# Sliding windows on one Trainium2 core: a second batch half stored four elements further on, and tiles that leave by two queues

## The chip, the cores and the metric

The kernel runs on one core of a Trainium2 chip. The metric is the device time of one launch in microseconds (us), median of the runs. Before the change it was 185.79 us over three runs (185.7 to 185.88). The profile is of one execution that took 186.0 us, of which the instruction span is 184.2 us.

The engines that matter here are VectorE (DVE in the profile), ScalarE (ACT), GpSimd (POOL) and SyncE (SP). POOL and SP issue the transfers; POOL writes the descriptors of its own in software (queue q0 in the profile), SP and ACT have theirs generated by hardware (q1 and q10). All transfers run on the same sixteen DMA engines of the core.

## The reference

```python
n_h = (h - window_size) // stride + 1
n_w = (w - window_size) // stride + 1
for i in range(n_h):
    for j in range(n_w):
        result[:, i, j] = x[:, :, i*stride : i*stride + window_size, j*stride : j*stride + window_size]
```

`x` is (16 batches, 64 channels, 64, 64) in float32, the window is 8 by 8 and the stride 4, so the result is (16, 15, 15, 64, 8, 8). Nothing is computed but addresses: 16.78 MB are read, and each element is written up to four times, 58.98 MB in all. One window of one batch, all channels, is a row of 64 x 8 x 8 x 4 bytes = 16 KB that is contiguous in the output; there are 16 x 15 x 15 = 3600 such rows.

## The kernel before

**The image in SBUF.** Tile `L` holds the whole input. A partition holds one quarter of the image height (16 rows of 64, `HQ` = 4 quarters) of one batch, for one half of the channels (32, `CL`). Partition number = 64 x channel half + 4 x batch + quarter. So batches 0 to 7 (the half `y` = 0) are partitions 0 to 31 and 64 to 95, and batches 8 to 15 (`y` = 1) the other 64. The rows of a channel are padded from 1024 to 1056 elements.

**Loading.** The first eight channels of each half come as full 16-partition transfers into staging `S` (which shares memory with the output tiles) by SP and ACT, and are copied into `L` on VectorE and ScalarE (line 135). The others come straight into `L` by `load` (line 59): eight partitions and one quarter at a time, 4 KB per channel; ten large and six small ones on POOL's queue and six on SP's. The POOL ones wait for each other in a ring of eight completion semaphores.

**Output tiles.** There are four buffers `G` of 128 partitions x 16 KB, used in turn. A partition of a tile holds one output row. A quarter of the height starts four windows (`NSLOT` slots, s = 0 to 3); slot 3 crosses into the next quarter, and its lower four image rows are fetched from the next partition by a shuffle on VectorE (line 170) with mask `nxt`. The last quarter has no slot 3.

The tiles are of these kinds, in program order:
- `part(y, j)`, six of them: slots 0 and 1 of columns j and j+1 for one batch half, so that storing can start before the second batch half has been loaded. Eight copies of 32 partitions each.
- `unit(j, 0)`: slots 0 and 1 of one column, all batches, one slot in each half of the partitions. Eight of them.
- `unit(j, 2)`, fifteen of them: slots 2 and 3 of one column. One half of the tile is copied by ScalarE; the other half is slot 3 and takes VectorE shuffles. After the early part, copies on VectorE are written as shuffles with an identity mask (`shf`, line 177), and ScalarE takes a share (`mix`, line 181).
- two last half tiles for column 14, slots 0 and 1, on partitions 32 to 95 (lines 246 to 256), that leave by SP.

**Stores.** All tiles but the last two leave by `scatter` (line 147): POOL reads a table of row numbers, one per partition, and writes one 16 KB row for each. A row number beyond the end of the output is skipped; that is how the missing slot 3 of the last quarter is left out (16 partitions in each of the fifteen `unit(j, 2)`). The stores are declared free of order among each other, so only reuse of a buffer waits for a store.

The order on each engine is the order in which the code emits the instructions. The main loop emits three `unit(j, 2)` and then one `unit(j, 0)`, five times.

Of the kernel before, what the change touches and what calls it, by code (L numbers as in the profile page):

```python
# [10 lines left out]
def kernel(  # L11
# [19 lines left out]
    CH = 2  # L31
# [18 lines left out]
    PAD = W // 2  # L50
    Lt = lpool.tile([P, CL, RB * W + PAD], f32)
    L = Lt[:, :, 0 : RB * W].rearrange("p c (r w) -> p c r w", r=RB)
    x_v = x.rearrange("(y b) (ch cl) (hq r) w -> ch y hq b cl (r w)", y=NY, ch=CH, hq=HQ)
# [3 lines left out]
    SMALL, HWP = 4, 6  # L57
# [10 lines left out]
    pi, tb, tq, tc_, th, idx, idx_y0, idx_y1, idx_lo, idx_hi = (  # L68
        itile(n) for n in ("pi", "tb", "tq", "tc", "th", "idx", "idx_y0", "idx_y1", "idx_lo", "idx_hi")
    )  # L70
    FAR = float(2 * B * NWIN)
    nc.gpsimd.iota(pi[:, :], pattern=[[0, 1]], base=0, channel_multiplier=1)  # L72
# [4 lines left out]
    def mul(d, a, m):  # L77
        nc.vector.tensor_scalar(out=d[:, :], in0=a[:, :], scalar1=float(m), scalar2=None, op0=ALU.mult)  # L78

    def tt(d, a, b, op):  # L80
        nc.vector.tensor_tensor(out=d[:, :], in0=a[:, :], in1=b[:, :], op=op)  # L81

    bits(tb, 2, B - 1)
    bits(tq, 0, HQ - 1)
    bits(tc_, 6, 1)
    mul(tb, tb, NWIN)
    mul(th, tq, NSLOT * NW)
    tt(tb, tb, th, ALU.add)
    mul(th, tc_, NW)
    tt(idx, tb, th, ALU.add)  # L90

    bits(th, 5, 1)
    mul(idx_y0, th, 1 - YB * NWIN)
    tt(idx_y0, idx_y0, idx, ALU.add)
    nc.vector.tensor_scalar(out=idx_y1[:, :], in0=idx_y0[:, :], scalar1=float(YB * NWIN), scalar2=None, op0=ALU.add)

    nc.vector.tensor_scalar(out=tq[:, :], in0=tq[:, :], scalar1=float(HQ - 1), scalar2=FAR, op0=ALU.is_equal, op1=ALU.mult)
    tt(th, tc_, tq, ALU.mult)
    tt(idx_hi, idx, th, ALU.add)
    nc.vector.tensor_scalar(out=tc_[:, :], in0=tc_[:, :], scalar1=-1.0, scalar2=1.0, op0=ALU.mult, op1=ALU.add)  # L100
    tt(th, tc_, tq, ALU.mult)
    tt(idx_lo, tb, th, ALU.add)
    mul(th, tc_, NW)
    tt(idx_lo, idx_lo, th, ALU.add)
# [26 lines left out]
    for n, (y, ch, c) in enumerate(first + then):  # L131
        f = slice(QP + y * QP, QP + (y + 1) * QP)
        d = slice(ch * HP + y * QP, ch * HP + (y + 1) * QP)
        copy = nc.vector.tensor_copy if n % 3 else nc.scalar.copy
        tc.keep_in_program_order(copy(out=L[d, c : c + PC, :, :], in_=S[ch][f, c : c + PC]))  # L135
# [3 lines left out]

    o_q = out.rearrange("b i j c r w -> i j b (c r w)")  # L140
# [17 lines left out]
    def fill(g, half, s, j, lo, n, copies):  # L158

        d = slice(half * HP + lo, half * HP + lo + n)  # L160
        cols = slice(j * ST, j * ST + WS)
        for ch in (half, 1 - half):
            f = slice(ch * HP + lo, ch * HP + lo + n)
            cs = slice(ch * CL, (ch + 1) * CL)
            copy = copies[ch != half]
            if s < NSLOT - 1:
                copy(out=g[d, cs, :, :], in_=L[f, :, s * ST : s * ST + WS, cols])  # L167
            else:
                copy(out=g[d, cs, 0:ST, :], in_=L[f, :, s * ST : RB, cols])
                nc.vector.stream_shuffle(out=g[d, cs, ST:WS, :], in_=L[f, :, 0:ST, cols], mask=nxt)  # L170

    act, dve = nc.scalar.copy, nc.vector.tensor_copy
    same = list(range(32))


    def shf(out, in_):
        nc.vector.stream_shuffle(out=out, in_=in_, mask=same)  # L177

    def split(k, other):
        def both(out, in_):  # L180
            act(out=out[:, 0:k], in_=in_[:, 0:k])  # L181
            other(out=out[:, k:], in_=in_[:, k:])  # L182

        return both

    mix = split(CL // 4, shf)


    EARLY = 3
    ACT_C = 12  # L190
# [7 lines left out]
    def part(y, j):  # L198
        g = tile_()
        order = [(d, ch) for ch in range(CH) for d in range(P // QP)]  # L200
        for n, (d, ch) in enumerate(order):
            s, dj = d // NY, d % NY
            cols = slice((j + dj) * ST, (j + dj) * ST + WS)
            f = (ch * NY + y) * QP
# [3 lines left out]
                    in_=L[f : f + QP, :, s * ST : s * ST + WS, cols],  # L208
# [4 lines left out]
    crossed = 0  # L213

    def unit(j, s, copies=(shf, mix)):
        nonlocal crossed
        g = tile_()
        if s == 0:
            fill(g, 0, 0, j, 0, HP, (act, copies[0]))
            fill(g, 1, 1, j, 0, HP, (act, copies[1]))  # L220
            scatter(g, idx, j, s)
        else:

            turn = 1 - crossed % 2
            crossed += 1
            fill(g, turn, s, j, 0, HP, (act, act))
            fill(g, 1 - turn, s + 1, j, 0, HP, (shf, mix))
            scatter(g, (idx_hi, idx_lo)[turn], j, s)
# [63 lines left out]
```

## Time and profile before

| what | value |
|---|---|
| median of three runs | 185.79 us (185.7 to 185.88) |
| profiled execution | 186.0 us, span 184.2 us |
| VectorE busy | 154.0 us (84%) in 213 instructions |
| ScalarE busy | 150.6 us (82%) in 100 |
| GpSimd busy | 50.3 us (27%) in 50 |
| DMA moved | 75.81 MB in 10980 packets, mean 411 GB/s |
| scatters | 29 of 128 partitions |
| SP stores | 2 of 64 partitions |

The profile's page cuts the span into 40 slices and gives the busy share of each engine in tenths, for the DMA engines too. Its groups of instructions give line, engine, operation, output and input, shape and count, then busy time, the mean of one in ns, and the idle time in front of them. A table by stage gives, for chosen stretches of the span, the busy time and the number of instructions of each engine, the granted clock of TensorE (not used here), the mean busy share of the DMA engines and what they moved. That busy share adds up the recorded packet times, which overlap a little, so it can read 1.01 or 1.03.

### The profile page before, as it was taken

The page shows a single profiled execution, that of the slowest core. Times are in us where ns is not written, and L with a number is a line of the kernel's source. Part 1 is how long each engine was busy: PE and PEld are TensorE (multiplying, and loading weights), DVE is VectorE, ACT ScalarE, POOL GpSimd, SP SyncE. Part 2 cuts the span into 40 slices and gives each one's busy share as a digit, 9 for nine tenths or more (in the row PEclk, how much of TensorE's full clock was granted, in tenths as well). Part 3 has the DMA queues.
Part 4 walks back from the last instruction along what each step waited for, and adds up shares of the span by engine and source line. Part 5 has one row for each costly group of instructions (what it writes and reads, how often), then busy time and mean ns, then how long its engine had stood idle before and what let it go on. Part 6 is the DMA issues. An engine that isn't in the chain of part 4 may idle for free.

```text
span 184.2 us, 597 instructions
## 1 busy us (share of the span) xinstructions
DVE 154.0 (84%) x213; ACT 150.6 (82%) x100; POOL 50.3 (27%) x50
## 2 busy tenths in 40 slices
DVE  5002998999989897999999999999999999999800
ACT  0002999999999999999899999998999999999600
POOL 7400763033353526111121112111211121114000
DMA  5999999999999999999999999999999999999995
GB/s 141 396 413 408 412 412 412 395 396 441 425 430 430 430 434 427 434 432 430 434 422 438 423 434 438 423 441 413 443 416 427 434 423 413 427 420 406 420 430 235
DMA packets 10980, 75.81 MB, mean 411 GB/s; under 512 B 3280, under 2 KB 3280, under 8 KB 7376
## 3 DMA queue, kind: packets, MB, share of 16 engines
q0 software_dynamic: 8656, 65.55, 84.8%
q1 hardware_dynamic: 1744, 8.13, 10.9%
q10 hardware_dynamic: 576, 2.10, 3.2%
q14 instruction: 4, 0.03, 0.0%
HBM read 16.78 MB, written 62.91 MB: 433 GB/s over the span
## 4 chain that ended last, share of the span: by engine, by line
DVE 53%; DMA 28%; issue 10%; POOL 2%; DVEq 1%; PEldq 0%
DVE GG L177 24%; DVE GG L170 16%; DMA out_dram<-GG,idx_y 14%; DMA Lt<-in_x_dram 14%; DVE GG L206 10%; DVE GG L254 3%; POOL Lt L61 2%; DVE GG L182 0%; DVEq L287 0%; DVE GG L167 0%; POOL pi L72 0%; DVEq L206 0%; PEldq L287 0%
## 5 line engine op out<-in xcount | busy, mean ns | idle before, releaser
L167 ACT COPY GG<-Lt 64x2048 f32<-64x2048 f32 x46 | 87.2, 1897 | 4.2 <-DMA out_dram<-GG,idx 1.8
L177 DVE STREAM_SHUFFLE GG<-Lt 64x1024 f32<-64x1024 f32 (+4 forms) x39 | 52.8, 1355 | 1.3
L206 DVE COPY GG<-Lt 32x2048 f32<-32x2048 f32 x30 | 36.6, 1219 | 3.4 <-DMA out_dram<-GG,idx_y 2.2
L170 DVE STREAM_SHUFFLE GG<-Lt 64x1024 f32<-64x1024 f32 x30 | 38.5, 1285 | 0.0
L206 ACT COPY GG<-Lt 32x2048 f32<-32x2048 f32 x18 | 34.1, 1897 | 0.8 <-DMA out_dram<-GG,idx_y 0.4
L135 DVE COPY Lt<-GG 32x2048 f32<-32x2048 f32 x10 | 11.9, 1234 | 13.8 <-DMA GG<-in_x_dram 13.7
L61 POOL DMA_DIRECT2D Lt<-in_x_dram x16 | 13.7, 868 | 17.8 <-DMA Lt<-in_x_dram 17.3
L147 POOL DMA_INDIRECT out_dram<-GG,idx_y x6 | 10.1, 1690 | 26.3 <-DVE GG L206 17.6
L147 POOL DMA_INDIRECT out_dram<-GG,idx x8 | 11.7, 1463 | 17.5 <-DVE GG L177 13.3
L147 POOL DMA_INDIRECT out_dram<-GG,idx_lo x8 | 7.7, 964 | 30.2 <-DVE GG L170 15.1
L135 ACT ACT_TABLE_LOAD x1 | 1.3, 1283 | 17.3 <-DMA GG<-in_x_dram 17.3
L147 POOL DMA_INDIRECT out_dram<-GG,idx_hi x7 | 6.7, 963 | 26.5 <-ACT GG L167 11.4
L135 ACT COPY Lt<-GG 32x2048 f32<-32x2048 f32 x6 | 11.2, 1894 | 0.1
L181 ACT COPY GG<-Lt 64x256 f32<-64x256 f32 (+2 forms) x21 | 10.2, 484 | 0.5
L167 DVE COPY GG<-Lt 64x2048 f32<-64x2048 f32 x6 | 7.3, 1222 | 0.2
L254 ACT COPY GG<-Lt 32x768 f32<-32x768 f32 x8 | 6.6, 828 | 0.1
L254 DVE COPY GG<-Lt 32x1280 f32<-32x1280 f32 x8 | 6.6, 819 | 0.1
L75 DVE TENSOR_SCALAR tb<-pi 128x1 int32<-128x1 int32 x1 | 0.2, 154 | 1.0 <-POOL pi L72 1.0
L182 DVE COPY GG<-Lt 64x1280 f32<-64x1280 f32 x1 | 0.9, 875 | 0.0
L81 DVE TENSOR_TENSOR th<-tc,tq 128x1 int32<-128x1 int32 x2 | 0.3, 156 | 0.0
L78 DVE TENSOR_SCALAR th<-tc 128x1 int32<-128x1 int32 x2 | 0.3, 154 | 0.0
L72 POOL IOTA pi<- 128x1 int32 x1 | 0.1, 125 | 0.4 <-PEq L287 0.4
(21 smaller groups left out, 3.1 us busy)
## 6 DMA issues: line engine op xcount, KB each, us to landing
Lt<-in_x_dram POOLq DMA_DIRECT2D x10, 768.0 KB, 17.9
Lt<-in_x_dram SPq DMA_DIRECT2D x6, 640.0 KB
GG<-in_x_dram SPq DMA_DIRECT2D x4, 512.0 KB, 14.8
GG<-in_x_dram ACTq DMA_DIRECT2D x4, 512.0 KB, 14.5
out_dram<-GG SPq DMA_DIRECT2D x2, 1024.0 KB, 9.5
Lt<-in_x_dram POOLq DMA_DIRECT2D x6, 128.0 KB, 17.8
out_dram<-GG,idx POOLq DMA_INDIRECT x8, 11.9
out_dram<-GG,idx_lo POOLq DMA_INDIRECT x8, 9.5
```

What stands on the lines that cost most here:

```text
L61: eng.dma_start(out=L[p0 : p0 + QP - HQ + 1 : HQ, c0:c1, :, :], in_=x_v[ch, y, q, :, c0:c1, :])
L78: nc.vector.tensor_scalar(out=d[:, :], in0=a[:, :], scalar1=float(m), scalar2=None, op0=ALU.mult)
L81: nc.vector.tensor_tensor(out=d[:, :], in0=a[:, :], in1=b[:, :], op=op)
L135: tc.keep_in_program_order(copy(out=L[d, c : c + PC, :, :], in_=S[ch][f, c : c + PC]))
L147: st = nc.gpsimd.indirect_dma_start(out=o_v, out_offset=bass.IndirectOffsetOnAxis(ap=ix[:, 0:1], axis=0), in_=g.rearrange("p c r w -> p (c ...
L167: copy(out=g[d, cs, :, :], in_=L[f, :, s * ST : s * ST + WS, cols])
L170: nc.vector.stream_shuffle(out=g[d, cs, ST:WS, :], in_=L[f, :, 0:ST, cols], mask=nxt)
L177: nc.vector.stream_shuffle(out=out, in_=in_, mask=same)
L181: act(out=out[:, 0:k], in_=in_[:, 0:k])
L182: other(out=out[:, k:], in_=in_[:, k:])
L206: (act if n % 3 == 0 else dve)(out=g[d * QP : (d + 1) * QP, ch * CL : (ch + 1) * CL, :, :], in_=L[f : f + QP, :, s * ST : s * ST + WS, cols],)
L254: copy(out=g[d, ch * CL + c0 : ch * CL + c1, :, :], in_=L[f, c0:c1, s * ST : s * ST + WS, cols])
```

## The change

It has four parts.

1. **The image.** Within each channel half the two batch halves change places (`lanes`): `y` = 1 is now partitions 0 to 31 and 64 to 95, `y` = 0 the others. The second batch half is written four elements (16 bytes, one column step) further on in each channel's row. There are two views of the same memory, `L[0]` and `L[1]`, four elements apart. Read through one view and for one set of columns, the partitions of one batch half give column j and those of the other give column j-1 or j+1.
2. **The tiles.** `unit(j, s)` now holds one slot. Its first 64 partitions are read through `L[0]` and its other 64 through `L[1]`. So its middle 64 partitions (32 to 95) hold slot s of column j for all sixteen batches in order, and its outer 64 hold column j-1 for `y` = 1 (partitions 0 to 31) and column j+1 for `y` = 0 (partitions 96 to 127). Units are made for even j. The middle leaves by SP: one plain store of 64 rows, or, for slot 3, three stores of 16 rows. The outer rows leave by the POOL scatter, whose table skips the middle rows, and at the edges (j = 0, j = 14 and, for slots 0 and 1, j = 6) one outer side as well. There are 8 units of slot 3, 8 of slot 2 and 10 of slots 0 and 1; with the six `part` tiles that is 32 tiles. The two last half tiles are gone.
3. **The copies.** A unit of slots 0 to 2 takes one ScalarE copy of 64 x 2048 elements, two of VectorE and one that is split in halves between both. A unit of slot 3 takes four ScalarE copies and four shuffles, all 64 x 1024. The shuffles with an identity mask are gone.
4. **Loads and tables.** The last load of channel half 0 is cut: its last four channels become two more POOL loads, of one and of three channels, that are issued last. There are more row-number tables, each by a few one-column operations on VectorE.

```diff
-    L = Lt[:, :, 0 : RB * W].rearrange("p c (r w) -> p c r w", r=RB)
+    L = [Lt[:, :, n * ST : n * ST + RB * W].rearrange("p c (r w) -> p c r w", r=RB) for n in range(2)]
...
+    def lanes(ch, y):
+        p0 = ch * HP + (NY - 1 - y) * QP
+        return slice(p0, p0 + QP)
+
+    SMALL, HWP, EVEN = 4, 6, 3
 
     def load(eng, ch, y, q, c0, c1):
-        p0 = ch * HP + y * QP + q
-        eng.dma_start(out=L[p0 : p0 + QP - HQ + 1 : HQ, c0:c1, :, :], in_=x_v[ch, y, q, :, c0:c1, :])
+        p0 = lanes(ch, y).start + q
+        eng.dma_start(out=L[y][p0 : p0 + QP - HQ + 1 : HQ, c0:c1, :, :], in_=x_v[ch, y, q, :, c0:c1, :])
...
-            load(nc.gpsimd, 0, y, q, FC, FC + SMALL if hw else CL)
+            end = FC + SMALL if hw else CL
+            if y * HQ + q == NY * HQ - 1:
+                end -= EVEN + 1
+            load(nc.gpsimd, 0, y, q, FC, end)
             load(nc.gpsimd, 1, y, q, FC, CL)
+
+    load(nc.gpsimd, 0, NY - 1, HQ - 1, CL - EVEN - 1, CL - EVEN)
+    load(nc.gpsimd, 0, NY - 1, HQ - 1, CL - EVEN, CL)
...
-    ACT_C = 12
+    ACT_C = CL // 2
...
-    def unit(j, s, copies=(shf, mix)):
+    def unit(j, s):
         g = tile_()
...
+        lo = j > (2 * EARLY if s < 2 else 0)
+        hi = j < NW - 1
+        cross = s == NSLOT - 1
+        cols = slice(j * ST, j * ST + WS)
+        for h in range(CH):
+            a, b = (0 if lo else QP, HP) if h == 0 else (0, HP if hi else QP)
+            d = slice(h * HP + a, h * HP + b)
+            for n, ch in enumerate((h, 1 - h)):
+                f = slice(ch * HP + a, ch * HP + b)
+                cs = slice(ch * CL, (ch + 1) * CL)
+                if cross:
+                    act(out=g[d, cs, 0:ST, :], in_=L[h][f, :, s * ST : RB, cols])
+                    nc.vector.stream_shuffle(out=g[d, cs, ST:WS, :], in_=L[h][f, :, 0:ST, cols], mask=nxt)
+                else:
+                    copy = (act, dve, dve, split(ACT_C))[h * CH + n]
+                    copy(out=g[d, cs, :, :], in_=L[h][f, :, s * ST : s * ST + WS, cols])
+        g_q = g.rearrange("p c r w -> p (c r w)")
+        if cross:
+            for q in range(HQ - 1):
+                free(nc.sync.dma_start(out=o_e[j, :, s + q * NSLOT], in_=g_q[QP + q : QP + HP - HQ + 1 + q : HQ]))
         else:
...
+            free(nc.sync.dma_start(out=o_e[j, :, s : s + (HQ - 1) * NSLOT + 1 : NSLOT], in_=g_q[QP : QP + HP]))
+        outer = ((sw, sx), (sw_lo, sx_lo), (sw_hi, sx_hi))[0 if lo and hi else 1 if lo else 2]
+        scatter(g, outer[cross], j, s)
 
     for n in range(EARLY):
         part(0, 2 * n)
-    plain = [(j, 0) for j in range(2 * EARLY, NW - 1)]
-    cross = [(j, 2) for j in range(NW)]
+    last = NW - 1
+    js = [2, last, 0, *range(4, last, 2)]
+    below = [(j, NSLOT - 2) for j in js]
+    cross = [(j, NSLOT - 1) for j in js]
+    js = list(range(2 * EARLY + 2, last, 2))
+    plain = [(j, s) for j in js[:-1] for s in range(2)]
+    plain += [(j, s) for s in range(2) for j in (last, 2 * EARLY, js[-1])]
     for n in range(EARLY):
-        unit(*plain.pop(0), (dve, dve))
+        unit(*plain.pop(0))
         part(1, 2 * n)
-    while plain:
-        for w in cross[:3]:
-            unit(*w)
-        cross = cross[3:]
-        unit(*plain.pop(0), *([] if len(plain) else [(split(ACT_C, shf), split(ACT_C, dve))]))
...
+    while cross:
+        unit(*cross.pop(0))
+        unit(*below.pop(0))
+        if len(plain) > len(cross):
+            unit(*plain.pop(0))
```

More of the change, by code (lines that the diff above doesn't have):

```diff
@@ L156, in scatter, with split @@
         free(st)
[L158 to L170, printed above, removed]
     act, dve = nc.scalar.copy, nc.vector.tensor_copy
[L173 to L179, printed above, removed]
+    def split(k):
         def both(out, in_):
             act(out=out[:, 0:k], in_=in_[:, 0:k])
-            other(out=out[:, k:], in_=in_[:, k:])
+            dve(out=out[:, k:], in_=in_[:, k:])
         return both
-    mix = split(CL // 4, shf)
     EARLY = 3
-    ACT_C = 12
+    ACT_C = CL // 2
     at = 0
@@ L211, in part @@
         scatter(g, (idx_y0, idx_y1)[y], j, 0)
[L213 to L216 removed]
+    o_e = out.rearrange("b i j c r w -> j b i (c r w)")
+    def unit(j, s):
         g = tile_()
[L218 to L221, printed above, removed]
[L222 to L228 removed]
+        lo = j > (2 * EARLY if s < 2 else 0)
[18 more added lines that the diff above has]
+                free(nc.sync.dma_start(out=o_e[j, :, s + q * NSLOT], in_=g_q[QP + q : QP + HP - HQ + 1 + q : HQ]))
+        else:
+            free(nc.sync.dma_start(out=o_e[j, :, s : s + (HQ - 1) * NSLOT + 1 : NSLOT], in_=g_q[QP : QP + HP]))
+        outer = ((sw, sx), (sw_lo, sx_lo), (sw_hi, sx_hi))[0 if lo and hi else 1 if lo else 2]
+        scatter(g, outer[cross], j, s)
```

77 lines of the change are left out of this document (32 added, 45 removed).

## The prediction

> **What bounds the kernel now.** I read the page's slices and queues first, because a kernel that only moves data can be no faster than its DMA engines.
>
> ```profile
> span 184.2 us, 597 instructions
> DVE 154.0 (84%) x213; ACT 150.6 (82%) x100; POOL 50.3 (27%) x50
> DMA  5999999999999999999999999999999999999995
> q0 software_dynamic: 8656, 65.55, 84.8%
> q1 hardware_dynamic: 1744, 8.13, 10.9%
> q10 hardware_dynamic: 576, 2.10, 3.2%
> ```
>
> The three queues add up to 98.9% of sixteen engines' span, 182.2 of 184.2 us. What is left is 2.0 us, about the start before the first packet. So taking waits away can win at most some 2 us; more needs shorter packets. The bytes stay the same.
>
> Second, the table by stage: busy times, then clock, DMA share and GB/s.
>
> ```profile
> 55.00:79.00 24.00, 21.82 (x21) 23.68 (x14) 9.21 (x5) 1.00 1.01 431
> 98.00:134.00 36.00, 35.47 (x55) 34.65 (x26) 7.69 (x8) 1.00 1.01 431
> 134.00:152.00 18.00, 17.70 (x27) 16.73 (x12) 3.28 (x5) 1.00 1.01 428
> 152.00:160.00 8.00, 7.91 (x15) 7.89 (x6) 1.58 (x2) 1.00 1.00 420
> 160.00:168.00 8.00, 7.88 (x13) 7.32 (x8) 1.93 (x2) 1.00 0.99 416
> 168.00:176.00 8.00, 6.06 (x8) 5.52 (x7) 1.04 (x1) 1.00 0.99 416
> ```
>
> Stores run at 431 GB/s, 16384 x 16 / 431 = 0.608 us for a row on one engine, and lose rate from 134 us on. From 134 to 176 us the mean is (18 x 428 + 8 x 420 + 16 x 416) / 42 = 421.9: a loss of 42 x (1 - 421.9/431) = 0.9 us. In those stages VectorE is 98% busy. The timeline shows why it matters; these lines are the scatters of successive `unit(j, 0)`.
>
> ```profile
> 95.98 0.96 POOL L147 DMA_INDIRECT out_dram<-GG,idx  x1 [3.25 <-DVE GG L177]
> 114.58 0.97 POOL L147 DMA_INDIRECT out_dram<-GG,idx  x1 [3.40 <-DVE GG L177]
> 133.06 0.97 POOL L147 DMA_INDIRECT out_dram<-GG,idx  x1 [3.26 <-DVE GG L177]
> ```
>
> A cycle of three slot-2 tiles and one slot-0 tile is filled in 18.55 us, but holds 3 x 112 + 128 = 464 rows, 29 per engine or 17.6 us of DMA. VectorE feeds 0.9 us too slowly per cycle and the DMA lives on its backlog. The issues of two stretches (55 to 79 us, 160 to 175 us), us from issue to landing last:
>
> ```profile
> out_dram<-GG,idx POOLq DMA_INDIRECT x2, 14.1
> out_dram<-GG,idx_hi POOLq DMA_INDIRECT x1, 8.6
> ```
>
> The backlog shrinks from 14.1 to 8.6 us and lasts just long enough. So DMA bounds the kernel, with VectorE almost level.
>
> **The change, part by part.** Prices per instruction, by shape:
>
> ```profile
> L167 ACT COPY GG<-Lt 64x2048 f32<-64x2048 f32 x46 | 87.2, 1897 | 4.2 <-DMA out_dram<-GG,idx 1.8 <-DMA out_dram<-GG,idx_hi 0.6 <-DMA out_dram<-GG,idx_y 0.6
> L170 DVE STREAM_SHUFFLE GG<-Lt 64x1024 f32<-64x1024 f32 x30 | 38.5, 1285 | 0.0
> L167 DVE COPY GG<-Lt 64x2048 f32<-64x2048 f32 x6 | 7.3, 1222 | 0.2
> L181 ACT COPY GG<-Lt 64x256 f32<-64x256 f32 x15 | 6.0, 402 | 0.3
> L147 POOL DMA_INDIRECT out_dram<-GG,idx_lo x8 | 7.7, 964 | 30.2 <-DVE GG L170 15.1 <-ACT GG L167 11.4 <-issue 3.8
> L147 POOL DMA_INDIRECT out_dram<-GG,idx_y x6 | 10.1, 1690 | 26.3 <-DVE GG L206 17.6 <-ACT GG L167 4.4 <-DMA Lt<-in_x_dram 4.4
> ```
>
> *Copies.* A 1024-element ScalarE copy lies on the line between 402 and 1897 ns: 1.04 us; VectorE's, between the 1222 of 2048 and the 875 of 1280 (line 182), about 0.75. A unit of slots 0 to 2 takes VectorE 2 x 1.22 + 0.75 = 3.2 us and ScalarE 2.9; one of slot 3 takes four shuffles, 5.1, and 4.2. A cycle of one slot 3, one slot 2 and one plain unit is 11.5 us of VectorE against 96 + 128 + 128 = 352 rows, 22 per engine, 13.4 us of DMA. VectorE leaves the edge, and in the early part it has 5 x 1.22 + 3.2 = 9.3 us per pair of tiles against 9.7 of DMA. Both hide under DMA, so the copies save nothing directly. What they can win is the late 0.9 us: between 0 and 0.9, as nothing shows whether thin backlog or the addresses stretched those packets; I take half, **-0.45 us**.
>
> *Skipped rows.* 26 units issue 26 x 128 = 3328 row numbers. Valid: 3600 rows less 768 of the `part` tiles less 18 x 64 + 8 x 48 = 1536 of the middles = 1296. So 2032 are skipped, 240 before: 112 more per engine. The trace lists a skipped row as a 4-byte packet of 9 ns, so at most 112 x 9 ns = 1.0 us; at least nothing, since these two stretches (55 to 79 and 79 to 103 us) move the same bytes with 80 and 129 packets under 512 B:
>
> ```profile
> DMA packets 712, 10.36 MB, mean 431 GB/s; under 512 B 80, under 2 KB 80, under 8 KB 80
> DMA packets 762, 10.36 MB, mean 431 GB/s; under 512 B 129, under 2 KB 129, under 8 KB 129
> ```
>
> 49 of them are only 0.03 us per engine there, too few to tell. I take the middle, **+0.5 us**.
>
> *More transfers.* SP issues 18 + 3 x 8 = 42 stores instead of 2, POOL 32 scatters instead of 29: 43 more completions per engine at 0 to 9 ns, 0 to 0.4, taken at **+0.2 us**. SP needs about 0.8 us per issue (four loads in 3.15), 34 us in all, and waits 152.6 us for VectorE today: hidden. Behind an SP store that waits for its tile only later SP stores are queued.
>
> *Loads.* Two more POOL loads at 0.87 us each stand ahead of the first scatter, and the second must wait for the tenth load's landing. The first scatter slips from 36.8 to about 39 us. Its rows start only when the loads have drained, at about 45 us, so it costs nothing; without that cover 2 us. 8 x 24 x 8 = 1536 of the 4096 load packets now land 16 bytes further on in SBUF, which no row shows. Odd channels already start at an odd multiple of 128 bytes (a channel is 4224 bytes), and the trace shows no second duration among the 4 KB packets: most take 159 to 162 ns, the slow tail some 167. So between nothing and 1536 x 8 ns / 16 = 0.8 us; nearest to the odd channels, I take **+0.1 us**; a real penalty is a rival. The new tables are some 0.15 us each on VectorE, idle until 17.35 us.
>
> *Buffers and uneven tiles.* A buffer is free when its SP stores and its scatter have both landed. Edge units store 32 outer rows instead of 64, all on one side of the tile: half of the engines have less to do. I take **+0.2 us**; how it could be more is below.
>
> Sum: -0.45 + 0.5 + 0.2 + 0.1 + 0.2 = +0.55 us. The profiled execution's 186.0 us is its span of 184.2 and 1.8 around it, and lies 0.2 above the median; from the median 185.79 this gives **186.3 us**.
>
> **The rivals.**
>
> *Faster.* If the skipped rows and completions cost nothing, as the stretches above allow, and the deeper backlog brings back all of the late 0.9 us, it ends at 184.9; the stage from 176 to 183 us has a DMA share of 0.89, 0.8 us idle, and with half of that too it ends at 184.5. It decides by whether stores after 134 us keep 431 GB/s. For it: fill 11.5 under 13.4. Against: the same rows by the same engines.
>
> *Half of the engines starve.* Column 14's slots 3 and 2 come one behind the other. One half of the engines gets 3 + 4 = 7 rows, the other 6 + 8 = 14: 7 x 0.608 = 4.3 us less work, while the buffers come free at the slower half's pace. Column 0 then mirrors it. The cover is the backlog: some 10 us from issue to landing less 4.9 for the tile's own rows and about 1 of latency, 4 us, level with the need. With half of the cover 2.1 us are lost: 188.5; with none 4.3: 190.6.
>
> [...]
>
> *Descriptors late.* Scatters beside VectorE copies (idx_y) took 1.69 us in the mean, beside shuffles (idx_lo) 0.96, and this change puts copies back. 0.7 us per scatter is hidden under the 4 us of cover, as between 55 and 79 us, where copies ran and DMA kept 431 GB/s. If cover were gone at the eight edge units, 8 x 0.7 / 2 (half of a tile is SP's) = 2.8: 189.1.
>
> [...]
>
> *Shifted loads are slow.* If the 16 bytes cost a tenth of a packet, 1536 x 0.016 / 16 = 1.5 us: 187.8 in the place of 186.3.
>
> **How the numbers follow.** About 0.2% (0.37 us) is what a measurement of this kernel can tell from no change, so the same is 185.42 to 186.16. Forecast 0.40 (0.25 slower, 0.12 the same, 0.03 faster: its terms span -0.9 to +2.2), faster rival 0.28 (0.26 faster, 0.02 the same), starved half 0.20, late descriptors 0.05, slow shifted loads 0.07 (all slower). Together faster 0.29, same 0.14, slower 0.57. The range reaches from 184.4, the faster rival's end less the runs' spread of 0.1, to 189.0, which leaves out the late descriptors and the worst of the starved half.
>
> **What would show it.** Right: DMA share 0.98 or more, VectorE near 152 us busy, packets under 512 B near 5800, stores at 431 GB/s after 134 us if the late loss was backlog. Wrong: store stages under 425 GB/s with share 1.0 (skipped rows cost more), or a share under 0.95 around 100 to 125 us (a starved half), or loads under 400 GB/s before 45 us (the shift).

## The result

The changed kernel took 240.19 us in the median of four runs (239.92 to 240.36), the kernel before 185.75 us beside it: 1.293 times as long (95% interval 1.291 to 1.295). The forecast of 186.3 us is 54 us too low, and the range, up to 189.0, ends 51 us below the measured time. The profiled execution took 240.15 us, its span 238.2.

The page of the changed kernel, the lines that answer to those shown of the kernel before:

```profile
span 238.2 us, 692 instructions
DVE 148.0 (62%) x183; ACT 132.9 (56%) x93; POOL 60.5 (25%) x55
DMA  6999999999999994571981992980993884596493
DMA packets 13493, 75.82 MB, mean 318 GB/s; under 512 B 5792, under 2 KB 5792, under 8 KB 9888
q0 software_dynamic: 9120, 42.49, 43.8%
q1 hardware_dynamic: 3792, 31.20, 31.6%
q10 hardware_dynamic: 576, 2.10, 2.4%
```

The same bytes are moved, and the three queues now add up to 77.8% of the engines' span instead of 98.9%. The slices show where the rest is. Up to slice 15 the DMA engines are full, as before; from there on to the end they pause every few slices. The engines that fill the tiles are not late either: VectorE is busy for 148.0 us (the forecast had 152), in a longer span. So the transfers and the copies have hardly become dearer: they have stopped running beside each other.

The table by stage says the same (columns: stretch, its length, busy time and instructions of VectorE, ScalarE and GpSimd, clock, DMA share, GB/s):

```profile
60.00:80.00 20.00, 16.64 (x17) 15.46 (x10) 5.22 (x4) 1.00 1.01 432
80.00:100.00 20.00, 10.40 (x16) 9.08 (x9) 2.87 (x3) 1.00 0.70 297
140.00:160.00 20.00, 11.36 (x14) 10.05 (x8) 3.80 (x3) 1.00 0.73 302
200.00:220.00 20.00, 11.58 (x15) 10.30 (x9) 3.78 (x3) 1.00 0.64 262
```

In most stretches of 20 us after 80 us VectorE is busy for 11 us, ScalarE for 10 and the DMA engines for 13 to 15: each of them waits for the others. The waits name the transfer (engine, tile and line, what it waited for, us in total, times, longest):

```profile
ACT GG L224 <- DMA out_dram<-GG: 67.9, 8, 10.8
DVE GG L224 <- DMA out_dram<-GG: 56.7, 8, 9.3
```

Eight waits of ScalarE and eight of VectorE, all at the copy of a slot-2 tile (line 224), all released by the landing of a store that SP issued (`out_dram<-GG`, without a row-number table). There are eight slot-3 units, and a slot-2 tile comes behind each. Two of the eight in the timeline (start, duration, engine and line, and in brackets the idle time before):

```profile
84.80 3.43 SPq L228 DMA_DIRECT2D out_dram<-GG  x3
85.50 0.96 POOL L159 DMA_INDIRECT out_dram<-GG,sx  x1 [4.28 <-DVE GG L221]
94.02 1.90 ACT L224 COPY GG<-Lt 64x2048 f32<-64x2048 f32 x1 [10.75 <-DMA out_dram<-GG]
...
137.90 1.79 SPq L228 DMA_DIRECT2D out_dram<-GG  x3
138.60 0.96 POOL L159 DMA_INDIRECT out_dram<-GG,sx  x1 [4.28 <-DVE GG L221]
143.07 1.90 ACT L224 COPY GG<-Lt 64x2048 f32<-64x2048 f32 x1 [6.69 <-DMA out_dram<-GG]
143.12 2.48 DVE L224 COPY GG<-Lt 64x2048 f32<-64x2048 f32 x2 [5.29 <-DMA out_dram<-GG]
```

SP issues the three 16-row stores of a slot-3 tile (`x3`, line 228), and the copies of the next tile start only when these have landed. But the next tile lies in another one of the four buffers, and the program's copies wait on exactly the three completion semaphores (the counters by which a transfer reports that it has landed) of the stores just issued: in the trace's records, the three stores of 84.80 us raise semaphores 101, 111 and 112, the last of them at 93.92 us, and the copies at 94.02 us wait for these three. The section on the kernel before says that only reuse of a buffer waits for a store; here that doesn't hold. The source of these stores, `g_q[QP + q : QP + HP - HQ + 1 + q : HQ]`, is every fourth partition of one buffer, and all four buffers are slices of one tile, `GG`.

### The profile page after: what moved, and what is told of

Read it like the earlier page. It is cut to its first block, busy times and chain, and to the rows that moved or that the text cites. A ratio compares the mean times of both kernels' runs of the same rounds, so it can differ in the third digit from the quotient of the medians.

```text
span 238.2 us, 692 instructions
## 1 busy us (share of the span) xinstructions
DVE 148.0 (62%) x183; ACT 132.9 (56%) x93; POOL 60.5 (25%) x55
## 2 busy tenths in 40 slices
DMA packets 13493, 75.82 MB, mean 318 GB/s; under 512 B 5792, under 2 KB 5792, under 8 KB 9888
## 3 DMA queue, kind: packets, MB, share of 16 engines
HBM read 16.78 MB, written 92.27 MB: 458 GB/s over the span
## 4 chain that ended last, share of the span: by engine, by line
DMA 43%; DVE 34%; issue 11%; SPq 6%; POOL 1%; DVEq 1%; POOLq 1%; PEldq 0%
DMA out_dram<-GG 17%; DMA Lt<-in_x_dram 16%; DVE GG L224 14%; DVE GG L221 12%; DMA out_dram<-GG,sw 10%; SPq L228 6%; DVE GG L175 4%; DVE GG L195 4%; POOL Lt L66 1%; POOLq L281 1%; DVEq L281 0%; DVEq L224 0%; POOL pi L74 0%; DVEq L221 0%; PEldq L281 0%
## 5 line engine op out<-in xcount | busy, mean ns | idle before, releaser
L224 DVE COPY GG<-Lt 64x2048 f32<-64x2048 f32 (+1 forms) x36 | 44.0, 1222 | 57.5 <-DMA out_dram<-GG 56.7
L224 ACT COPY GG<-Lt 64x2048 f32<-64x2048 f32 (+1 forms) x18 | 34.2, 1899 | 68.1 <-DMA out_dram<-GG 67.9
L221 DVE STREAM_SHUFFLE GG<-Lt 64x1024 f32<-64x1024 f32 (+1 forms) x32 | 40.7, 1273 | 1.2
L195 DVE COPY GG<-Lt 32x2048 f32<-32x2048 f32 x30 | 36.6, 1219 | 4.0 <-DMA out_dram<-GG,idx_y 2.9
L159 POOL DMA_INDIRECT out_dram<-GG,sw x12 | 18.1, 1508 | 66.2 <-DVE GG L175 62.1
L220 ACT COPY GG<-Lt 64x1024 f32<-64x1024 f32 (+1 forms) x32 | 33.4, 1043 | 0.8
L66 POOL DMA_DIRECT2D Lt<-in_x_dram x18 | 15.9, 898 | 21.4 <-DMA Lt<-in_x_dram 20.9
L174 ACT COPY GG<-Lt 64x1024 f32<-64x1024 f32 (+1 forms) x18 | 18.8, 1043 | 0.4
L175 DVE COPY GG<-Lt 64x1024 f32<-64x1024 f32 (+1 forms) x18 | 12.3, 686 | 0.6
L159 POOL DMA_INDIRECT out_dram<-GG,sx x6 | 5.8, 960 | 25.7 <-DVE GG L221 25.7
L159 POOL DMA_INDIRECT out_dram<-GG,sw_hi x3 | 3.8, 1261 | 11.4 <-DVE GG L175 8.7
L159 POOL DMA_INDIRECT out_dram<-GG,sw_lo x3 | 3.8, 1263 | 10.2 <-DVE GG L175 7.5
```

The lines of the kernel that those rows point to most:

```text
L66: eng.dma_start(out=L[y][p0 : p0 + QP - HQ + 1 : HQ, c0:c1, :, :], in_=x_v[ch, y, q, :, c0:c1, :])
L159: st = nc.gpsimd.indirect_dma_start(out=o_v, out_offset=bass.IndirectOffsetOnAxis(ap=ix[:, 0:1], axis=0), in_=g.rearrange("p c r w -> p (c ...
L175: dve(out=out[:, k:], in_=in_[:, k:])
L195: (act if n % 3 == 0 else dve)(out=g[d * QP : (d + 1) * QP, ch * CL : (ch + 1) * CL, :, :], in_=L[y][lanes(ch, y), :, s * ST : s * ST + WS ...
L220: act(out=g[d, cs, 0:ST, :], in_=L[h][f, :, s * ST : RB, cols])
L221: nc.vector.stream_shuffle(out=g[d, cs, ST:WS, :], in_=L[h][f, :, 0:ST, cols], mask=nxt)
```

## The experiments

The theories that the expectations name: A, a false wait (the strided read of the one tile is taken to overlap the other buffers); B, the 16-row SP stores are slow or expensive in themselves; C, the halves of the engines are loaded unevenly by the edge tiles; D, GpSimd's end lies bare behind a last scatter; E, the order of the edge tiles. Every experiment was compared with runs of the kernel before on the same chip (medians 185.62 to 185.81 us). The last column is the span of the profiled execution, from which packets, waits and stages are read; in `apart`, `near16` and `endsp` that execution took 1.7, 6.3 and 0.9 us longer than the median.

| run | median, us | ratio to before (95%) | span, us |
|---|---|---|---|
| `apart` | 193.53 | 1.042 (1.041 to 1.044) | 193.3 |
| `near16` | 217.42 | 1.173 (1.167 to 1.178) | 221.9 |
| `half` | 231.80 | 1.249 (1.246 to 1.251) | 229.4 |
| `allpool` | 192.79 | 1.038 (1.036 to 1.040) | 191.2 |
| `edges` | 191.86 | 1.033 (1.032 to 1.035) | 190.1 |
| `spread` | 192.29 | 1.036 (1.034 to 1.037) | 190.2 |
| `endsp` | 192.23 | 1.035 (1.033 to 1.036) | 191.4 |
| `tail` | 196.52 | 1.058 (1.057 to 1.060) | 194.7 |
| `tailsp` | 195.46 | 1.052 (1.051 to 1.054) | 193.4 |
| `nosk` | 282.85 | 1.522 (1.520 to 1.524) | 281.0 |
| `skips` | 193.03 | 1.039 (1.038 to 1.041) | 191.1 |
| `shift` | 186.53 | 1.004 (1.003 to 1.006) | 184.8 |

### Is the wait a false one? Four buffers as four tiles

`apart` is the changed kernel with nothing else touched but that each buffer is a tile of its own. The staging loads, which ran across two buffers, are cut in two.

```diff
-    GG = gpool.tile([P, NG, GF], f32)
-    G = [GG[:, n].rearrange("p (c r w) -> p c r w", c=C, r=WS) for n in range(NG)]
+    GT = [gpool.tile([P, GF], f32, name=f"G{n}") for n in range(NG)]
+    G = [t.rearrange("p (c r w) -> p c r w", c=C, r=WS) for t in GT]
```

> The four output buffers are four tiles instead of four slices of one tile; the staging loads are cut in two each to fit. Stores, copies and tables are those of the changed kernel. Theory A (the three SP stores of a slot-3 tile read every fourth partition of the one tile that holds all buffers, and the next tile's first copies, in another buffer, are made to wait until these stores have landed): the 67.9 us that ScalarE waits for SP stores fall under 10, and the time is 185 to 189 us. Theory B (the sixteen-row stores themselves are slow, or SP issues them too slowly): stores unchanged, so about 240. Theory C (the edge tiles' uneven halves starve half of the engines): tiles unchanged, so above 225.

It took 193.53 us, and its stages from 60 to 100 us are full:

```profile
60.00:80.00 20.00, 19.41 (x18) 16.45 (x11) 7.49 (x4) 1.00 1.01 422
80.00:100.00 20.00, 19.42 (x26) 16.96 (x14) 7.13 (x5) 1.00 1.01 421
```

The same three stores of the same partitions, and of 240.19 us 46.7 are gone; the view of waits has none for an SP store any more. Theory A is shown. The time is still 4.5 us above the 185 to 189 that A was expected to give, and the other three runs of this kind came out above their ranges for A too: A was the large cost and not the only one. Which rule of the program's dependency tracking makes these waits isn't in the traces.

### Is it the strided source, and how much does each one cost?

`near16` keeps the one tile and lets the three stores read 16 neighbouring partitions, so that these rows of the output hold other windows. `half` keeps the strided form in four of the eight slot-3 units and has the neighbouring form in the other four.

```diff
-                free(nc.sync.dma_start(out=o_e[j, :, s + q * NSLOT], in_=g_q[QP + q : QP + HP - HQ + 1 + q : HQ]))
+                free(nc.sync.dma_start(out=o_e[j, :, s + q * NSLOT], in_=g_q[QP + q * B : QP + (q + 1) * B]))
```

```diff
+                if j % 4 == 2:
+                    free(nc.sync.dma_start(out=o_e[j, :, s + q * NSLOT], in_=g_q[QP + q : QP + HP - HQ + 1 + q : HQ]))
+                else:
+                    free(nc.sync.dma_start(out=o_e[j, :, s + q * NSLOT], in_=g_q[QP + q * B : QP + (q + 1) * B]))
```

> The changed kernel, but the three SP stores of a slot-3 tile read sixteen neighbouring partitions each instead of every fourth one. Same number of stores, same bytes, same output rows, one tile for all buffers; the rows of these stores hold other windows than the reference has there. A: no wait for another buffer's stores, 186 to 192 us (neighbouring partitions may be read less evenly). B: same number and size of stores, about 240. C: above 225.

> The changed kernel with every fourth partition read by the SP stores of four of the eight slot-3 tiles (columns 2, 14, 6 and 10) and sixteen neighbouring partitions by those of the other four; those rows hold other windows than the reference has there. A: half of the loss, between 208 and 218 us. B and C: about 240.

`near16` has none of the eight waits, yet took 217.42 us. Its DMA engines are full, at a lower rate:

```profile
60.00:80.00 20.00, 16.68 (x16) 15.47 (x10) 5.73 (x4) 1.00 1.01 428
80.00:100.00 20.00, 15.65 (x20) 13.14 (x12) 4.73 (x4) 1.00 1.01 324
```

A row that SP stores took 854 ns in the mean of all 1536 SP rows there, 622 in the changed kernel. Only 8 x 48 = 384 of them are read from neighbouring partitions. The 384 longest took 1577 ns in the mean and the other 1152 took 613; the trace doesn't say which row belongs to which store, but in `half`, with 192 such rows, the 192 longest took 1599 ns and the others 616. By this estimate a row read that way took about 1.6 us. Why such a row takes longer isn't in the traces.

In `half` exactly four waits are left:

```profile
ACT GG L224 <- DMA out_dram<-GG: 39.9, 4, 11.5
DVE GG L224 <- DMA out_dram<-GG: 35.7, 4, 10.5
```

Four strided units, four waits; eight, eight; none in `near16`, `apart` or `allpool`. The 18 SP stores of 64 neighbouring partitions, out of the same tile, make no such wait in `near16` or `allpool`. So the trigger is the partition stride in the source of an SP store whose tile also holds the other buffers. The total of 231.80 us lies between 217.42 and 240.19, 3 us off the middle, and far above the 208 to 218 expected, since the rows of the other four units cost time of their own.

### Without the 16-row stores

`allpool` lets the middle rows of slot 3 leave by the scatter too. The tables hold their row numbers; nothing else changes.

```diff
-        if cross:
-            for q in range(HQ - 1):
-                free(nc.sync.dma_start(out=o_e[j, :, s + q * NSLOT], in_=g_q[QP + q : QP + HP - HQ + 1 + q : HQ]))
-        else:
+        if not cross:
```

> The changed kernel, but the middle rows of a slot-3 tile leave by the scatter together with the outer ones, so no SP store of sixteen rows is left; eight SP stores fewer per eight tiles times three. A: 185 to 189 us. B: also 185 to 189. C: above 225, since tiles and edges are the same.

192.79 us, close to `apart`, so the 24 small stores cost next to nothing by themselves once nobody waits for them, and theory B falls. What is left over the kernel before is 7.0 us of span. The packets of the traces divide it (us; rows and loads are the sums of packet times over sixteen engines, idle is the time between first and last packet in which engines had no packet of 4 KB or more, as a mean of sixteen, so that the 4-byte packets of skipped rows and completions lie in it; packets overlap a little, so the three parts add up to some 1 us more than the whole above them):

| | before | after | `apart` | `allpool` | `edges` |
|---|---|---|---|---|---|
| first to last packet | 180.8 | 232.7 | 187.9 | 185.8 | 184.7 |
| 16 KB rows | 138.2 | 139.7 | 140.4 | 139.5 | 139.5 |
| 4 KB load packets | 42.1 | 42.3 | 42.9 | 42.5 | 42.2 |
| engines idle | 1.8 | 51.7 | 5.7 | 5.0 | 4.2 |
| last packet to end | 1.3 | 3.3 | 3.2 | 3.2 | 3.2 |

The false wait is the 51.7 - 5.0 = 46.7 us of idle engines. The other 7 are 3.2 us of idle engines, 1.3 of longer rows, 0.4 of longer load packets and 2.0 at the end. Of the 3.2, engines had no packet at all for 2.6; in the other 0.6 they had small packets only, of which `allpool` has more, mostly skipped rows.

### The idle engines: uneven halves

The landings of `allpool` show the starved half of the forecast's rival: eight of the sixteen completions of a scatter come some 4 us behind the other eight. The scatter issued at 100.5 us had eight completions at 106.8 to 107.0 us and the others at 111.3 to 112.3. That the rows of one side of a tile leave by eight of the sixteen engines shows in the changed kernel. The rows of a full unit's scatter, issued at 98.01 us, start in groups of sixteen (the first two at 101.11 to 101.24 and 101.72 to 101.84), the 32 rows of an edge unit's, issued at 112.03, in four groups of eight (the first two at 115.14 to 115.34 and 115.76 to 115.95). The first scatter has its sixteen completions at 103.92 to 104.08 us, the second eight at 115.86 to 115.97 and eight at 118.00 to 118.22. The stages (of `allpool`):

```profile
100.00:120.00 20.00, 17.61 (x23) 16.36 (x14) 5.49 (x5) 1.00 0.95 394
120.00:140.00 20.00, 18.22 (x23) 15.54 (x14) 7.80 (x6) 1.00 0.94 390
140.00:160.00 20.00, 17.91 (x22) 14.96 (x12) 6.11 (x5) 1.00 1.00 414
```

`edges` orders the edge units so that tiles that lack opposite sides follow each other; `spread` puts the four edge units of slots 2 and 3 into separate rounds of the loop (it starts from `endsp`, below).

```diff
-    below = [(j, NSLOT - 2) for j in js]
+    below = [(j, NSLOT - 2) for j in [2, 0, last, *range(4, last, 2)]]
...
+    plain[3:6] = [plain[4], plain[5], plain[3]]
```

> The version in which the middle rows of slot-3 tiles leave by the scatter (192.8 us), with the edge tiles in another order: slot 3 of column 14 is followed by slot 2 of column 0 and the other way round, and the plain tiles of columns 14 and 6 follow each other, so that one half of the engines is never more than 4 rows behind the other instead of 7. Theory E (the uneven halves of the edge tiles starve one half of the engines between 100 and 135 us, about 3 us of DMA time): 189.5 to 191.5 us, with DMA shares of 0.98 and more from 100 to 140 us. If the order does not matter, 192.4 to 193.2.

```diff
-    below = [(j, NSLOT - 2) for j in [2, 0, last, *range(4, last, 2)]]
-    cross = [(j, NSLOT - 1) for j in js]
+    below = [(j, NSLOT - 2) for j in (0, 2, 4, 6, 8, 10, last, 12)]
+    cross = [(j, NSLOT - 1) for j in (2, 4, 6, last, 0, 8, 10, 12)]
```

> As the run before, and the four edge units of slots 2 and 3 no longer come near each other but one in each of the loop's rounds 1, 4, 5 and 7, mostly with the missing side alternating. Edge units take VectorE as long as full ones for fewer rows, and load one half of the engines. Theory C (it is the row of edge tiles that leaves engines idle between 100 and 130 us, 2.0 us more there than elsewhere): idle engines fall from 4.2 to 2 to 3 us, and the time is 1.2 to 2.2 us under that of the run before, 187.7 to 189.1. If the idle time there has another cause, the time is within 0.5 us of the run before.

`edges` gained 0.9 us, less than expected. Its stage from 100 to 120 us is no better than that of `allpool`, and shows a second thing about edge units: VectorE is 97% busy there.

```profile
100.00:120.00 20.00, 19.35 (x25) 17.22 (x15) 7.57 (x5) 1.00 0.92 380
120.00:140.00 20.00, 18.39 (x25) 16.57 (x14) 7.31 (x5) 1.00 1.00 415
```

An edge tile has a quarter of its rows less, but its copies and shuffles take as long, for fewer partitions at the same length (in the changed kernel a shuffle of 32 partitions took 1270 ns, of 64 partitions 1273, a VectorE copy of 2048 elements 1219 and 1223, a ScalarE copy 1899 both). In `spread` the engines' idle time between 90 and 130 us is 1.1 us against 3.0 in `endsp` and 2.3 in `edges`, as theory C has it; in its stages the share is 1.00 and more:

```profile
100.00:120.00 20.00, 17.81 (x23) 15.36 (x13) 6.84 (x5) 1.00 1.00 414
120.00:140.00 20.00, 18.27 (x23) 16.69 (x15) 8.71 (x5) 1.00 1.02 419
```

But 0.8 us of it came back between 170 us and the end. The profiled executions are 1.2 us apart in span, the medians not at all (192.29 against 192.23; that of `endsp`, 193.14 us, was its longest). That is the time that was expected if the gap had another cause. So the place of the gap is shown to depend on the edge tiles; that removing it pays is not.

### The end: GpSimd waits for its own queue

The last instruction of GpSimd is a DRAIN, which ends behind the last packet of its scatters. It is no busy time on the page; its records and the packets (us from the span's start; a scatter's last packet can be a small one) read:

| | last packet of a scatter | last packet of an SP store | end of GpSimd's DRAIN | span |
|---|---|---|---|---|
| before | 180.51 | 182.97 | 182.91 | 184.23 |
| `allpool` | 187.97 | 185.48 | 190.41 | 191.20 |
| `edges` | 186.89 | 184.39 | 189.29 | 190.09 |
| `endsp` | 187.99 | 187.97 | 190.57 | 191.36 |
| `spread` | 186.84 | 186.82 | 189.45 | 190.24 |
| `tail` | 191.71 | 165.44 | 193.94 | 194.74 |
| `tailsp` | 181.16 | 191.90 | 183.53 | 193.42 |

It ends 2.2 to 2.6 us behind the last scatter's last packet. The kernel before hides this under its two last half tiles, which leave by SP; the changed kernel ends with a scatter and pays 2.0 us. Three runs try to move it. `tail` is the kernel before with the half tiles made ahead of the last group, so that a scatter is last. `tailsp` is `edges` with the last two units leaving wholly by SP (the code is that of `nosk`, below, for these two alone). `endsp` is `edges` with the last unit made as two tiles, the scattered outer rows first.

```diff
     for n in range(EARLY):
         ...
     while plain:
+        if len(plain) == 1:
+            halves()
```

> The kernel before, with its two last half tiles moved ahead of the last group of tiles, so that the last transfer is a scatter. Theory D (after its last scatter has landed GpSimd takes some 2 us to drain; before, the stores of the two half tiles by SP cover it, and in every version of the changed kernel nothing does): GpSimd ends about 2 us behind the last landing and the time is 187.0 to 188.2 us. If the drain is hidden or moves with the load, 185.4 to 186.2.

> The version with the reordered edge tiles (191.9 us, span 190.1), but the last two units leave wholly by SP (their outer 32 partitions as plain stores too), so the last scatter is that of the last slot-3 unit. Theory D (GpSimd's end, 2.0 to 2.5 us after the last scatter's packets, lies bare at the end): it goes under the last SP stores, 189.3 to 190.2 us. If the end costs nothing of its own: 191.5 to 192.0. The packets between 60 and 160 us should not change.

```diff
-            unit(*plain.pop(0))
+            end = len(plain) == 1
+            w = plain.pop(0)
+            for side in ("outer", "middle") if end else (None,):
+                unit(*w, side)
```

> The version with the reordered edge tiles (191.86 us; its last packet, a scatter's, ends 3 us before the span does), with the last unit made as two tiles: the outer rows first, by the scatter, then the middle rows, by SP. The same rows, one tile more. Theory D (the end of GpSimd's queue lies bare when the last transfer is a scatter): the end behind the last packet shrinks from 3.0 to about 1.0 to 1.3 us, as where SP stores come last, and the time is 189.7 to 190.4. If the end is as long behind any last transfer: 191.6 to 192.2.

None of the three times says it cleanly: those of `tail` and `tailsp` lie outside of both ranges, and that of `endsp` lies where no gain was expected. In `tail`, 196.52 us, a ScalarE copy that needs the first half tile's buffer ran ahead of copies of earlier tiles, and ScalarE and VectorE stood still:

```profile
163.64 5.60 ACT L167 COPY GG<-Lt 64x2048 f32<-64x2048 f32 x3 [8.93 <-DMA out_dram<-GG]
171.52 0.96 POOL L147 DMA_INDIRECT out_dram<-GG,idx_lo  x1 [19.13 <-DVE GG L170]
173.61 0.96 POOL L147 DMA_INDIRECT out_dram<-GG,idx_lo  x1 [1.13 <-DVE GG L170]
178.33 0.97 POOL L147 DMA_INDIRECT out_dram<-GG,idx_hi  x1 [3.76 <-ACT GG L181]
```

The code emits the scatters of this last group in the order `idx_lo`, `idx_hi`, `idx_lo`; they ran in another. So the section on the kernel before is not right that the order on each engine is always the order of emission; the code pins only some copies to it, with `keep_in_program_order`. But the end of `tail` is as theory D has it: the span ends 3.0 us behind the last packet, a scatter's, where that of the kernel before ends 1.3 us behind an SP store's. In `tailsp`, 195.46 us, the end behind the last packet (191.9) shrank to 1.5 us, as theory D has it too, but the stores of 32 rows put it later, for the reason that the next run shows. In `endsp`, 192.23 us, the last 16 KB row of the scatter ended only 0.7 us ahead of the last SP row and its last packet together with SP's, and the DRAIN ended the span all the same. What is shown is the place and the size: the span ends 1.3 to 1.5 us behind the last packet where SP stores come well after the last scatter, and 3.0 to 3.4 where they don't. That a kernel's time gains these 2 us is not shown by any run.

### A store of 32 partitions runs on eight engines

`nosk` is `edges` with all units of slots 0 to 2 leaving by SP alone, the outer 32 partitions as plain stores. It was meant to take away 1344 skipped rows and the uneven halves.

```diff
+        if not cross:
+            if lo:
+                free(nc.sync.dma_start(out=o_e[j - 1, YB:, s : s + (HQ - 1) * NSLOT + 1 : NSLOT], in_=g_q[0:QP]))
+            if hi:
+                free(nc.sync.dma_start(out=o_e[j + 1, 0:YB, s : s + (HQ - 1) * NSLOT + 1 : NSLOT], in_=g_q[P - QP : P]))
+            return
```

> As the run before, but all eighteen units of slots 0 to 2 leave wholly by SP; only slot 3 and the six part tiles are scattered. 1344 skipped rows fewer, 84 per engine, at 5 ns 0.4 us. Edge units of slots 0 to 2 are no longer one-sided if an SP store of 32 rows spreads over all sixteen engines. Theory C (uneven halves cost most of the 4.2 us of idle engines): idle falls to 2 to 3 us, and the time with D's 2 us to 187.2 to 188.9. If C is small and only D and the skipped rows count: 189.0 to 189.8. If rows are longer for another reason than these, their mean stays near 620 ns against 614 before, 1.3 us of what is left over the kernel before.

282.85 us, far outside of all that was expected. The DMA share in its stages is near a half or two thirds:

```profile
120.00:140.00 20.00, 12.31 (x15) 11.06 (x9) 2.64 (x2) 1.00 0.54 226
140.00:160.00 20.00, 11.89 (x15) 9.10 (x8) 1.32 (x1) 1.00 0.66 217
```

In `tailsp`, where nothing else is in flight at the end, the rows of these stores start in groups of eight every 0.61 us, not sixteen. Those of a 64-row store of the middle, in the changed kernel with idle engines, start in groups of sixteen (98.55 to 98.70 us, 99.16 to 99.31, 99.77 to 99.92, 100.41 to 100.56). An outer store is eight batches by four rows in the output, a middle one sixteen by four; what sets the number of engines isn't in the traces. That some eight engines carry more than the other eight shows in `nosk`: the full scatter issued at 154.6 us has eight completions at 161.6 to 161.7 us and the other eight at 168.4 to 168.6. So the uneven load that the scatter had at the edge tiles alone was in every tile of slots 0 to 2 here. If both outer sides go by the same eight, the 960 outer rows of these stores are 120 for each of eight engines instead of 60 for each of sixteen: 60 x 0.61 = 37 us of the 91 us over `edges`, an estimate. Rows were also longer (685 ns in the mean against 620, 225 x 65 ns = 15 us); the rest is not divided here.

### The small terms: skipped rows and the shift

`skips` is the kernel before with one more scatter behind each of its 23 units, with a table that skips all 128 rows: 184 skipped rows per engine and nothing stored. `shift` is the kernel before with the whole image 16 bytes further on (3072 load packets instead of 1536).

```diff
+    nc.vector.tensor_scalar(out=none[:, :], in0=pi[:, :], scalar1=1.0, scalar2=FAR, op0=ALU.mult, op1=ALU.add)
...
         scatter(g, idx, j, s)
+        scatter(Lf, none, j, s)
```

> The kernel before, with one more scatter behind each of the 23 unit tiles, all of whose 128 row numbers are skipped: 2944 more skipped rows, 184 per engine, from partitions that no later copy writes. If a skipped row takes an engine's 9 ns on top of the rows, 187.0 to 187.9 us; if skipped rows hide beside rows, 185.5 to 186.3.

```diff
-    L = Lt[:, :, 0 : RB * W].rearrange("p c (r w) -> p c r w", r=RB)
+    L = Lt[:, :, ST : ST + RB * W].rearrange("p c (r w) -> p c r w", r=RB)
```

> The kernel before, with the whole image four elements (16 bytes) further on in SBUF, so that all 3072 load packets that go there directly land on the shifted address. The changed kernel shifts 1536. If a shifted packet takes 5 ns longer (as the mean of the load packets says, 165.8 against 164.4 ns over all 4096), 3072 x 5 / 16 = 1.0 us: 186.4 to 187.0. If the shift costs nothing, 185.4 to 186.0.

`skips` took 193.03 us, 7 us over the kernel before, which neither expectation has. Its packets divide that into 2.2 us of idle engines (as in the table above), 1.9 of longer rows (622 instead of 614 ns) and 2.8 at the end, where its last all-skipped scatters stand. In a stretch of 10 us from 110 us on, where 22 small packets per engine came on top, idle time grew by 0.13 us, 5.8 ns for each; three more stretches of 10 us around it give 4.5 to 5.7 ns. At 5 ns, 184 of them are 0.9 us. That agrees with the forecast's 4.5 ns as the gap that a skipped row leaves. Nothing was added here but scatters that skip all their rows, and rows became 8 ns longer, so skipped rows may be what lengthens the rows of `allpool` too. But that is not settled: rows were at 611 to 613 ns up to 100 us here though the skipped rows came from 60 us on, and at 622 to 637 between 100 and 180; the kernel before has 615 to 621 after 130 us.

`shift` took 186.53 us, 0.4% more, as expected for a shift that costs something. The mean of a load packet rose from 164.4 to 167.2 ns, (2.8 x 4096) / 3072 = 3.7 ns for each shifted one, and 2.8 x 256 = 0.7 us in all.

## Why the prediction was wrong, step by step

- **The step that failed** is "A buffer is free when its SP stores and its scatter have both landed". It takes for granted that only the same buffer waits. The four buffers are one tile, and behind each strided store the next buffer's copies waited for it as well: eight times, 46.7 us of idle DMA engines. The term "Buffers and uneven tiles", 0.2 us, is where that cost would have stood. No rival had it. The forecast had asked of each new wait who stands behind it, on SP's queue only, and had not asked whom the new reads make wait. In the trace of before the only SP stores read 64 partitions without a stride and come last, so no row there showed it.
- **Uneven tiles**, in the same term, were mis-sized too: engines without any packet for 2.6 us more in `allpool` than before, all of it between 100 and 140 us (2.7 us against 0.0). The rival of the starved half (188.5, or 190.6 without cover) had the mechanism, the place (100 to 125 us, share under 0.95; it was 0.95 and 0.94) and the size of the lag, 4.3 us (measured 4.3 and more). It lacked that an edge tile also takes VectorE as long as a full one. The 1 us of latency in its cover agrees with the changed kernel: the issue of an SP store that found idle engines ended at 97.89 us, its first row started at 98.55, its last ended at 101.21, and it had landed at 101.63, 1.1 us in all beside the rows. How the 2.6 us divide between the two stays open.
- **The late rate**, -0.45 us, went the other way: rows took 619.9 ns in the mean of `allpool` and not 614.1, 225 x 5.8 ns = +1.3 us. Between 140 and 160 us scatters there took 11.3 to 13.4 us from issue to landing, against 8.8 to 9.6 before, and rows took 627 ns against 618. So a deeper backlog did not bring 611 ns back, and thin backlog was not what stretched them. The cause is open (skipped rows are a candidate, by `skips`), and the faster rival's main support is gone.
- **Skipped rows**, +0.5 us, agree as gaps: 112 at some 5 ns are 0.6 in the changed kernel, and the 88 that `allpool` has (its scatters store 384 rows more) 0.4. Their number agrees too (5792 packets under 512 B, about 5800 forecast). If they also lengthen the rows beside them, as `skips` suggests, the term was too small; the forecast's sign for that, stages under 425 GB/s with a share of 1.0, is there in `allpool` (414 after 140 us).
- **Loads**, +0.1 us, were near 0.4 (1536 packets at 3.7 ns; 165.8 against 164.4 ns in `allpool`), inside the range of 0 to 0.8. The sign named for the shift, under 400 GB/s before 45 us, is just there: 399 from 30 to 45 us, 408 before. The odd channels were the wrong neighbour to price it by. The rival of slow shifted loads, 1.5 us, falls.
- **The end** had no term: 2.0 us. The forecast noted that the half tiles go, but not that they cover GpSimd's DRAIN.
- **More transfers**, +0.2 us: not measured apart. `apart` has 24 SP stores more than `allpool` and took 0.7 us longer, also with its staging loads cut in two and 384 more skipped rows, so these effects are known only together.
- **Copies** were near: 1024-element copies took 1043 ns on ScalarE and 686 on VectorE (1.04 and 0.75 forecast), VectorE 148 us busy (152), and they would hide, as the full stages of `apart` show. The late descriptors are there as longer scatters, 1508 ns beside copies against 960 beside shuffles, and nothing shows that they cost time:

```profile
L159 POOL DMA_INDIRECT out_dram<-GG,sw x12 | 18.1, 1508 | 66.2 <-DVE GG L175 62.1
L159 POOL DMA_INDIRECT out_dram<-GG,sx x6 | 5.8, 960 | 25.7 <-DVE GG L221 25.7
L220 ACT COPY GG<-Lt 64x1024 f32<-64x1024 f32 (+1 forms) x32 | 33.4, 1043 | 0.8
```

Two readings of the kernel before were loose, without weight in the sum. VectorE is 98% busy from 134 to 168 us, but not in the last of the stages named (6.06 of 8 us). And the 2.0 us left beside the queues' shares is not only the start: the first packet begins at 2.2 us and the last ends 1.3 us before the span does, and packets overlap in between.

With the false wait taken away the change would still have been some 7 us slower (`allpool`), or 6 in the best order tried (`edges`), none of it from one large term. No version tried beats the kernel before.

## What to carry to other kernels

When a store gets a partition stride, ask what else lies in the same tile: buffers that are slices of one tile can be made to wait for each other (here eight times, 46.7 us of idle DMA engines), and the waits' view shows it as copies that wait for a transfer out of a buffer that they don't write. Buffers that are used in turn are safer as separate tiles (`apart` took 193.53 us, the changed kernel 240.19). A forecast that costs a change at some tenths of a microsecond because everything hides under DMA has to check, of each new access, that it leaves the overlap itself alone; what is at stake there is the whole of the hidden work. And what runs last matters by its queue: behind a scatter this program's end took some 2 us longer than behind SP's stores, though no run here turned that into a gain.

## What was not expected of the hardware

- GpSimd's closing DRAIN ends 2.2 to 2.6 us behind the last packet of its scatters (seven traces; 3.3 in `skips`).
- In `near16`, where 24 stores read 16 neighbouring partitions each, the longest 384 rows of 16 KB, as many as are read that way, took 1577 ns in the mean and the other SP rows 613; with every fourth partition, in the changed kernel, all SP rows took 622.
- A plain store from SP whose rows are eight batches by four ran on eight engines, and in `nosk`, with two such stores in each full tile of slots 0 to 2, the DMA share was 0.54 to 0.66 between 120 and 160 us.
- A 16-byte shift of the destination cost 3.7 ns for each 4 KB load packet of 164 ns.
- The page counts a skipped row as written with its full 16 KB, though its packet has 4 bytes. This line is of the kernel after; 58.98 MB of output and 2032 x 16 KB = 33.29 MB make its 92.27. It is not traffic: the packets moved 75.82 MB, reads and writes together.

```profile
HBM read 16.78 MB, written 92.27 MB: 458 GB/s over the span
```
